# Layer 1 with its projections token-major, gates turned by TensorE, and six places for split weights

## The chip, the cores and the metric

The kernel runs on one core of one Trainium2 chip, as one launch. A core has five engines with a queue each, which take their instructions in order: TensorE (PE in the profile, its weight loads PEld), VectorE (DVE), ScalarE (ACT), GpSimd (POOL) and SyncE (SP), which here issues DMAs. The metric is the device time of that core in microseconds, the median of several runs.

## The reference, cut to what matters

Two layers over 256 latent tokens and 256 context tokens of width 2048, all in float32. Layer 0 runs neighbourhood attention and a bidirectional state-space scan and is not changed. Layer 1 is a short gated convolution over the latent tokens:

```python
shift, scale, gate = adaln(c, ada_w[i], ada_b[i])
h = modulate(rms_norm(x, norm_g[i]), shift[:, None], scale[:, None])
...
def short_conv_mixer(h, w_in, conv_w, w_out):
    p = h @ w_in
    bg, cg, hv, g = jnp.split(p, 4, axis=-1)
    y = bg * dw_conv(cg * hv, conv_w)
    return (jax.nn.silu(g) * y) @ w_out
...
x = x + gate[:, None] * y
```

`w_in` is 2048 x 8192 here, `w_out` 2048 x 2048, and `dw_conv` has three taps along the tokens for each channel.

## The kernel before

[...] Weights arrive in chunks of 512 KB (two blocks of 128 input channels by 512 columns) in a `raw` buffer (L377); ACT rounds them to the high part `wH` (L407), DVE subtracts for the low part `wL` (L414). There are three places for split chunks; `split` may run at most three chunks ahead of the use.

The program is written out in an order that the kernel works out while it is built. The main code emits the matmuls of a projection chunk by chunk and calls `pump` between them; side work stands in generators in the queues `urgent`, `side` and `back`. A generator yields what it needs (an engine and the tiles it reads, or a condition), and `pump` emits its next piece when the model `Plan` says that the engine will be free and the tiles ready. `force` emits until a condition holds. What comes out is one fixed order for each engine, which the chip runs in order; where the model was too hopeful an engine waits.

Two forms of projection are used. In the form "act" (`mm_act`) a block of activations, 128 channels by 128 tokens, is the stationary operand and 512 columns of weights stream through: tokens end up on the partitions, in one bank for each of the two token tiles, with three matmuls of 512 columns per block and tile. In the form "both" (`mm_both`) a block of weights, 128 channels by 128 columns, is stationary, and the high and low activations of all 256 tokens, side by side, stream through: 512 columns with the high weights, then 256 (high activations only) with the low weights. Channels end up on the partitions, with high and low terms in two halves of a bank that are added while it is evicted.

- Output projection of layer 0 ("act"): 32 blocks of `mix` by four column blocks of 512, in three passes. At its last pass the last three chunks (`NTAIL` 13 of 16) are run first for token tile 0, then for tile 1, so that the rows of tile 0 can be evicted early. `res_gen` (L1582 to L1589) multiplies by the gate, adds x to give `x1`, and sums the squares on ACT.
- Entry to layer 1. `turn_gen` turns `x1` to channel-major, two blocks at a time, by eight pieces of four transposes (L193), and multiplies by the norm's weight. `norm_gen` makes the factor of the norm for each tile (L1652, and POOL L1653), spreads it over the partitions by a transpose, and for each of 16 blocks multiplies (L1681 or L1683), rounds with the shift added (ACT L1688) and takes the rest (DVE L1669), for both token tiles together. `keep_up` gives PE 8 and 6 transposes of a constant to do. Layer 1's matmuls begin when the first blocks of both tiles are there. While `hold` is set no further weights are split but where `norm_gen` does so.
- Input projection of layer 1 ("both"): for each of four groups of 512 channels, the parts cg, hv, bg, g, four banks each, 16 blocks by four column blocks. Evictions: `both` copies one half (ACT L1771) and adds the other (DVE L1773); `hv_gen` multiplies by cg and runs the three taps along the free axis (L1786 to L1794); `bg_gen` multiplies (L1801); `gg_gen` does the gate by tanh (L1810 to L1814) and splits the product into `y2` (L1818, L1819).
- Output projection of layer 1 ("act"), evicted by `fin_gen` (L1840, L1842) with a store for each tile.
- In the background the modulation of layer 1 is computed from `ada_w` by DVE (L804, `acc`), with a few small matmuls; the last 36 of its 256 steps on DVE fall into layer 1's input projection.

Of the kernel before, what the change touches and what calls it, by code (L numbers as in the profile page):

```python
# [141 lines left out]
def kernel(ctx: ExitStack, tc, x, cx, ada0, ada_w, ada_b, w_in, w_out, sc_in, sc_out, rpb, small, const,  # L142
# [245 lines left out]

    def split():
        k = pos["split"]  # L390
        raw, v = RAW.pop(k)
        nb, n = v.shape[1], v.shape[2]
        if n == 64:

            while lows:
                low_part()
            W = WH[k % NW].rearrange("p (b c) -> p b c", b=nb)
# [7 lines left out]
        H = WH[k % NW][:, :nb * n].rearrange("p (b c) -> p b c", b=nb)  # L405
        Lo = WL[k % NW][:, :nb * n].rearrange("p (b c) -> p b c", b=nb)
        E(S.copy(H, v))  # L407
        lows.append((k, H, Lo, v, raw))
        pos["split"] += 1
# [13 lines left out]
    def split_half(b):  # L423
# [5 lines left out]
        def rest():  # L429
            E(V.tensor_tensor(out=Lo[:, b], in0=v[:, b], in1=H[:, b].bitcast(F32), op=ALU.subtract))  # L430
            if b:
                RAW.pop(0)
                HL[0] = (H, Lo)
                pos["split"] += 1
                give_raw(raw)
                issue()
# [3 lines left out]
    def splits_try():  # L440
# [3 lines left out]
        while pos["split"] < pos["use"] + NW and pos["split"] in RAW:  # L444
# [18 lines left out]
    def used():  # L463
        pos["use"] += 1
        splits_try()
# [78 lines left out]
    for i in range(4):  # L544
        for part in (1, 2, 0, 3):
# [104 lines left out]
    def mm_both(ps, act, H, Lo, first, last):  # L650

        for b, o in enumerate(ps):
            bb = slice(b * 128, (b + 1) * 128)
            mm(o, H[:, bb], act, first, False)
            mm(o[:, :256], Lo[:, bb], act[:, :256], False, last)
            if b % 2:
                pump()

    def chunk(kb0, kind, ps, first, last, lhs=None):
# [3 lines left out]
        for j in range(nb):  # L663
# [5 lines left out]
            elif kind == "both":  # L669
                mm_both(ps, aH, H[:, j], Lo[:, j], f, l)  # L670
# [896 lines left out]
    def res_gen(k, c0, ps):  # L1567
# [31 lines left out]
    rb1 = []  # L1599
# [5 lines left out]
    def turn_gen():  # L1605
        yield when(lambda: n_back[0] >= 11.5 and attn[0] == 32 and ssd_done[0] == 8)
        for k in range(2):
            pt = st([128, 4, 256], f"PT{k}", name=f"late{k}")
            late[4 * k:4 * k + 4] = [pt[:, q, :] for q in range(4)]
        E(V.scalar_tensor_tensor(out=A1, in0=M1[:, 1], scalar=1.0, in1=P_("g1"), op0=ALU.add, op1=ALU.mult))  # L1610
        for kp in range(0, KB, 2):
# [6 lines left out]
            if kp == 14:  # L1618
                keep_up(8)
                yield when(lambda: ("sq", 3, 1) in got)  # L1620
# [12 lines left out]
    def keep_up(n):  # L1633

        pt = bank()
        for _ in range(n):
            turn(pt[:, :128], ident)
        give(free_b, pt)

    s3 = st([128, 2], "s3")  # L1640

    def norm_gen():
# [4 lines left out]
        rb = None  # L1647
        for t in range(2):
            yield when(lambda: ("sq", 3, t) in got)
            yield W_("DVE", ss1[:, t])  # L1650
# [3 lines left out]
            ahead = t == 0 and pos["split"] < pos["use"] + NW and pos["split"] in RAW  # L1654
            if ahead:
                split()
            if ahead:
                while lows:
                    low_part()

            yield W_("PE", r, nb=0 if t else 1)
            if t == 0:
                rb = bank()
            turn(rb[:, t * 128:(t + 1) * 128], r.to_broadcast([128, 128]))
        keep_up(6)
        hls = {}

        def low(kb):
            E(V.scalar_tensor_tensor(out=hls[kb][:, 1], in0=late[kb], scalar=S1[:, kb:kb + 1], in1=hls[kb][:, 0].bitcast(F32),  # L1669
                                     op0=ALU.add, op1=ALU.subtract))  # L1670
            hL[kb] = hls[kb][:, 1]
            h1[kb] = hls[kb].rearrange("p a b -> p (a b)")


        base = pos["use"]
        r2 = None
        for kb in range(KB):
            yield when(lambda: ("turn", kb) in got and (kb < 6 or pos["use"] >= base + kb // 2 - 2))
            yield W_("DVE", rb if r2 is None else r2, held[kb] if kb in held else late[kb])
            if kb not in held:  # L1680
                E(V.tensor_tensor(out=late[kb], in0=late[kb], in1=rb[:, :256] if r2 is None else r2, op=ALU.mult))  # L1681
            else:
                E(V.scalar_tensor_tensor(out=late[kb], in0=held[kb][:, (kb % 2) * 256:(kb % 2) * 256 + 256], scalar=A1[:, kb:kb + 1],  # L1683
                                         in1=r2, op0=ALU.mult, op1=ALU.mult))
                if kb % 2:
                    give(free_b, held[kb])
            hls[kb] = st([128, 2, 256], f"hL{kb}", F32R, name=f"h1_{kb}")
            E(S.activation(hls[kb][:, 0], late[kb], AF.Identity, bias=S1[:, kb:kb + 1], scale=1.0))  # L1688
            if kb:
                low(kb - 1)  # L1690
            while lows and kb in (3, 5):
                low_part()
            if kb == 3:
                r2 = half()
                E(S.copy(r2, rb[:, :256]))
                give(free_b, rb)
            if kb in (1, 3) and pos["split"] < pos["use"] + NW and pos["split"] in RAW:
                split()
        low(KB - 1)
        give(free_h, r2)  # L1700

    NTAIL = 13
    kcol = 0
    for ns in ((0, 512), (1024,), (1536,)):
        pss = [banks(2) for n in ns]
        for ip in range(16):
# [8 lines left out]
            if hold[0]:  # L1715
# [4 lines left out]
                ws = [use(q) for q in range(16 - NTAIL)]  # L1720
                spawn(urgent, norm_gen(), 0, 1)
                for t in range(2):
                    for q, (H, Lo) in enumerate(ws):
                        for b in range(2):
                            i = 2 * order[NTAIL + q] + b
                            mm_act([pss[0][t]], mH[i][:, 0, t * 128:(t + 1) * 128], mH[i][:, 1, t * 128:(t + 1) * 128],
                                   H[:, b], Lo[:, b], False, NTAIL + q == 15 and b == 1)
# [8 lines left out]
        if len(ns) == 2:  # L1736
            force(lambda: attn[0] == 32 and not side)
            x1 += [st([128, D], "KT", name="x1a"), st([128, D], "Vt", name="x1b")]
            spawn(side, turn_gen())
# [10 lines left out]
    force(lambda: hL[1] is not None, (urgent,))  # L1750
    hold[0] = False
    pump()
# [4 lines left out]
    flat = lambda ap, b: ap[:, 2 * b:2 * b + 2, :].rearrange("p b c -> p (b c)")  # L1757
    cg, u, v = st([128, 4, 256], "gt", name="cg"), st([128, 4, 256], "sz", name="u"), st([128, 4, 256], "QT", name="v")
# [3 lines left out]
    def ordered(k, gen):  # L1762
        yield when(lambda: seq[0] == k)
        yield from gen
        seq[0] += 1

    def both(p, o=None):

        yield W_("ACT", p)
        o = half() if o is None else o  # L1770
        E(S.copy(o, p[:, 256:]))  # L1771
        yield W_("DVE", o)
        E(V.tensor_tensor(out=o, in0=p[:, :256], in1=o, op=ALU.add))  # L1773
        give(free_b, p)
        return o

    def cg_gen(i, ps):
        for b in range(4):
            yield from both(ps[b], cg[:, b, :])

    def hv_gen(i, ps):
        for b in range(4):
            ch = 4 * i + b
            yield from both(ps[b], u[:, b, :])
            yield W_("DVE", u[:, b, :])
            E(V.tensor_tensor(out=u[:, b, :], in0=u[:, b, :], in1=cg[:, b, :], op=ALU.mult))  # L1786
            yield W_("ACT", u[:, b, :])
            E(S.mul(v[:, b, :], u[:, b, :], scw[:, 1, ch:ch + 1]))
        for b in range(4):
            ch = 4 * i + b  # L1790
            yield W_("DVE", v[:, b, :])
            E(V.scalar_tensor_tensor(out=v[:, b, 1:256], in0=u[:, b, 0:255], scalar=scw[:, 0, ch:ch + 1], in1=v[:, b, 1:256],
                                     op0=ALU.mult, op1=ALU.add))
            E(V.scalar_tensor_tensor(out=v[:, b, 0:255], in0=u[:, b, 1:256], scalar=scw[:, 2, ch:ch + 1], in1=v[:, b, 0:255],  # L1794
                                     op0=ALU.mult, op1=ALU.add))

    def bg_gen(i, ps):
        for b in range(4):
            bg = yield from both(ps[b])
            yield W_("DVE", bg, v[:, b, :])  # L1800
            E(V.tensor_tensor(out=v[:, b, :], in0=bg, in1=v[:, b, :], op=ALU.mult))  # L1801
            give(free_h, bg)

    def gg_gen(i, ps):
        for b in range(4):
            kb = 4 * i + b
            gg = yield from both(ps[b])
            yield W_("ACT", gg)
            th = half()
            E(S.activation(th, gg, AF.Tanh, scale=0.5))  # L1810
            yield W_("DVE", v[:, b, :])
            E(V.tensor_tensor(out=v[:, b, :], in0=gg, in1=v[:, b, :], op=ALU.mult))
            yield W_("DVE", th)
            E(V.scalar_tensor_tensor(out=v[:, b, :], in0=th, scalar=1.0, in1=v[:, b, :], op0=ALU.add, op1=ALU.mult))  # L1814
            give(free_h, gg, th)
            yield W_("ACT", v[:, b, :])
            hl = st([128, 2, 256], f"hH{kb}", F32R, name=f"y2_{kb}")
# [95 lines left out]
```

## Time and profile before

| | us |
|---|---|
| median of 3 runs | 1796.73 (1795.94 to 1799.53) |
| profiled execution | 1797.29 |
| its span, first to last instruction | 1795.5 |
| granted TensorE clock, mean | 1.000 |
| first matmul of layer 1's input projection | 1337.51 |
| first matmul of its output projection | 1701.90 |

Times within the trace are microseconds from the span's start. In a row of the timeline stand start, length, engine, line, operation, output <- inputs, shapes and count; in brackets the idle time of the engine before it and what ended it. Matmuls of a run overlap in the trace (each is listed with its latency), so their cost is the distance from one start to the next.

### The profile page before, as it was taken

To read this page: it belongs to the slowest core of one execution; us is meant where nothing else is said; L and a number is where in the kernel's file an instruction comes from. 1 tells how busy PE (TensorE), PEld (TensorE's weight loads), DVE (VectorE), ACT (ScalarE), POOL (GpSimd) and SP (SyncE) were. 2 spreads that over 40 slices of the span, in tenths; PEclk is the share of its full clock that TensorE was granted. 3 is DMA by queue.
4 is the path that set the end of the run, shared out by engine and by line. 5 is a ranking of instruction groups with operands and counts; after the bars stand their busy time and mean duration, and the time that the engine had idled before them with its cause. 6 is when DMAs were issued, how large, how long until landed. Compare 5 with 4: busy or idle time off the path is not lost. (4 is left out here: it accounts for less than half of the span.)

```text
span 1795.5 us, 26501 instructions
## 1 busy us (share of the span) xinstructions
PE 1765.5 (98%) x10039; PEld 1490.7 (83%) x10039; DVE 1292.8 (72%) x2073; ACT 786.9 (44%) x1386; POOL 32.5 (2%) x28
## 2 busy tenths in 40 slices
PE   6999999999999999999999999999999999999998
PEld 4677988879888889888888898788888888888887
DVE  5656787888676878676877688786667877565665
ACT  5323544455242445242435344555444444444442
POOL 0000100001000000000001000000000000000000
PEclk9999999999999999999999999999999999999999
DMA  9987744666746665745764567657766786666564
GB/s 359 339 285 239 225 143 125 204 183 200 235 127 202 211 185 175 232 139 173 218 200 134 165 185 247 202 186 268 274 222 225 249 265 222 185 185 187 186 213 150
DMA packets 222368, 374.67 MB, mean 209 GB/s; under 512 B 32432, under 2 KB 69136, under 8 KB 222240
## 3 DMA queue, kind: packets, MB, share of 16 engines
q1 hardware_dynamic: 214928, 366.38, 64.0%
q10 hardware_dynamic: 7312, 6.61, 1.1%
q8 instruction: 78, 1.28, 0.3%
q14 instruction: 50, 0.41, 0.1%
HBM read 367.52 MB, written 6.72 MB: 208 GB/s over the span
## 5 line engine op out<-in xcount | busy, mean ns | idle before, releaser
L407 ACT CAST wH<-raw 128x1024 fp32r<-128x1024 f32 (+1 forms) x439 | 457.8, 1044 | 687.3 <-PE bank L189 561.3
L414 DVE TENSOR_TENSOR wL<-raw,wH 128x1024 fp32r<-128x1024 f32 (+1 forms) x439 | 531.5, 1214 | 250.0 <-ACT wH L407 247.2
L189 PE MATMUL bank<-h,wH 128*128 128x512 f32 x1024 | 362.5, 399 | 1.4 <-DVE h L1669 0.9
L189 PE MATMUL bank<-hH,wH 128*128 128x256 f32 (+1 forms) x1040 | 343.3, 330 | 0.8 <-ACT wH L407 0.8
L189 PE MATMUL bank<-hL,wH 128*128 128x256 f32 (+1 forms) x1040 | 338.0, 325 | 0.0
L189 PE MATMUL bank<-hH,wL 128*128 128x256 f32 (+1 forms) x1024 | 330.8, 323 | 0.8 <-DVE wL L414 0.6
L189 PE MATMUL bank<-h,wL 128*128 128x256 f32 x1024 | 287.6, 281 | 0.0
L189 PE MATMUL bank<-wH,hH 128*128 128x512 f32 x640 | 257.1, 402 | 3.9 <-ACT hH L744 2.6
L189 PE MATMUL bank<-wL,hH 128*128 128x512 f32 x640 | 250.4, 392 | 0.0
L189 PE MATMUL bank<-wH,hL 128*128 128x512 f32 x640 | 249.8, 391 | 0.1
L804 DVE SCALAR_TENSOR_TENSOR acc<-raw,csil,acc 128x512 f32<-128x512 f32 x256 | 191.8, 749 | 63.2 <-DMA raw<-in_ada_w 54.3
L189 PEld LDWEIGHTS bank<-h,wH 128*128 128x128 f32 x1024 | 192.4, 188 | 50.4 <-issue 1.5
L189 PEld LDWEIGHTS bank<-hH,wH 128*128 128x128 f32 x1040 | 196.5, 189 | 18.6 <-ACT wH L407 1.3
L189 PEld LDWEIGHTS bank<-hL,wH 128*128 128x128 f32 x1040 | 196.8, 189 | 15.5
L189 PEld LDWEIGHTS bank<-hH,wL 128*128 128x128 f32 x1024 | 194.0, 189 | 18.3 <-DVE wL L414 1.6
L189 PEld LDWEIGHTS bank<-h,wL 128*128 128x128 f32 x1024 | 193.4, 189 | 0.0
L189 PE MATMUL bank<-wH,mix 128*128 128x512 f32 x512 | 163.1, 393 | 1.1 <-DVE Vt L998 1.1
L189 PEld LDWEIGHTS bank<-wH,hH 128*128 128x128 f32 x640 | 120.2, 188 | 33.8 <-issue 5.0
L189 PEld LDWEIGHTS bank<-wH,hL 128*128 128x128 f32 x640 | 120.2, 188 | 26.1 <-DVE hL L750 0.6
L189 PEld LDWEIGHTS bank<-wL,hH 128*128 128x128 f32 x640 | 120.2, 188 | 24.7 <-DVE wL L430 0.5
L189 PEld LDWEIGHTS bank<-wH,mix 128*128 128x128 f32 x512 | 96.1, 188 | 21.7 <-DVE Vt L998 1.6
L189 PE MATMUL bank<-wL,mix 128*128 128x512 f32 x256 | 100.0, 391 | 0.3 <-DVE wL L414 0.3
(262 smaller groups left out, 1764.0 us busy)
## 6 DMA issues: line engine op xcount, KB each, us to landing
raw<-in_w_in SPq DMA_DIRECT2D x208, 512.0 KB
raw<-in_ada_w SPq DMA_DIRECT2D x128, 512.0 KB
raw<-in_sc_in SPq DMA_DIRECT2D x128, 512.0 KB
raw<-in_w_out SPq DMA_DIRECT2D x64, 512.0 KB
raw<-in_ada SPq DMA_DIRECT2D x37, 512.0 KB
raw<-in_sc_out SPq DMA_DIRECT2D x32, 512.0 KB
tmp<-dram_csr SPq DMA_DIRECT2D x32, 256.0 KB
PT<-in_ada SPq DMA_DIRECT2D x14, 512.0 KB
```

The source lines that it names most:

```text
L189: E(T.matmul(o, l, r, start=start, stop=stop, skip_group_check=True))
L407: E(S.copy(H, v))
L414: E(V.tensor_tensor(out=Lo, in0=v, in1=H.bitcast(F32), op=ALU.subtract))
L804: E(V.scalar_tensor_tensor(out=acc, in0=v[:, j], scalar=csil[:, 2 * k + j:2 * k + j + 1], in1=acc, op0=ALU.mult, op1=ALU.add))
```

## The change

The same sums of products are computed. The parts of layer 1's input projection change form, order and eviction; its entry is cut by token tiles; the number of places for split weights becomes six from the second of the three passes of layer 0's output projection on.

- Places are handed out from a list `free_w` and return when a chunk is used. The three new ones lie in tiles that are free by then: `KL`, `QT` with `QL`, and `gt` with `sz`.
- The input projection runs in the form "act", two banks for each part, in the order cg, hv, g, bg. cg is copied by ACT, hv multiplied by it on DVE, the gate is made from g (tanh on ACT, one multiply-add on DVE), all with tokens on the partitions. `over` turns the products by four transposes into one bank for two column blocks: u before the taps, and bg times the gate before it meets the taps' output.
- At the entry the first eight blocks are scaled, rounded and split for token tile 0 alone and layer 1's first 48 matmuls run on it; then the same for tile 1. Blocks 8 to 15 follow for both tiles, two at a time. The eviction of the second tile's rows of `x1` waits for "first". The transpose that spreads the first factor is emitted after 15 of the 18 last matmuls of tile 1 (`NSTOP`). `keep_up` is gone.

```diff
+    free_w, in_use = deque(range(NW)), deque()
+    def place():
+        in_use.append(free_w.popleft())
+        return in_use[-1]
...
-        while pos["split"] < pos["use"] + NW and pos["split"] in RAW:
+        while free_w and pos["split"] in RAW:
...
-        for part in (1, 2, 0, 3):
+        for part in (1, 2, 3, 0):
             q_proj(sc_in, part * D + i * 512, 512)
...
-            yield when(lambda: x1 and (k in passed or ("rows", k, t) in got))
+            yield when(lambda: x1 and (k in passed or ("rows", k, t) in got) and (k < 3 or t == 0 or "first" in got))
...
+        def scaled(kb, tt):
+            o = pts[kb // 4][:, kb % 4:kb % 4 + 2, tt]
+            E(V.tensor_tensor(out=o, in0=o, in1=rb[0][:, tt].unsqueeze(1).to_broadcast([128, 2, 128]), op=ALU.mult))
+            high(kb, tt)
+            high(kb + 1, tt)
...
+        yield from factor(0)
+        ahead()
+        yield from spread(0)
+        tt = slice(0, 128)
+        yield W_("DVE", rb[0][:, tt])
+        scaled(0, tt)
+        scaled(2, tt)
+        for kb in range(0, 4):
+            low(kb, tt)
+        scaled(4, tt)
+        got.add("first")
+        yield when(lambda: ("sq", 3, 1) in got)
+        low(4, tt)
+        low(5, tt)
+        scaled(6, tt)
+        yield from factor(1)
+        if lows:
+            low_half(0)
+        low(6, tt)
+        low(7, tt)
...
+        yield from spread(1)
...
+        yield from pair(8)
+        for kp in range(8, KB, 2):
+            if lows:
+                low_part()
+            low(kp, slice(0, 256))
+            low(kp + 1, slice(0, 256))
+            if kp < KB - 2:
+                yield from pair(kp + 2)
...
+            for H, Lo in ((KL[:, 0:2], KL[:, 2:4]), (QT, QL), (st([128, 4, 256], "gt", F32R, name="wH5"), st([128, 4, 256], "sz", F32R, name="wL5"))):
+                free_w.append(len(WH))
...
+    def over(rows_, b):
+        yield W_("PE", *rows_, nb=1)
+        pt = bank()
+        for k in range(2):
+            for t in range(2):
+                turn(pt[:, k * 256 + t * 128:k * 256 + (t + 1) * 128], rows_[t][:, (b + k) * 128:(b + k + 1) * 128])
+        return pt
...
+    def bg_gen(i, ps):
+        for t in range(2):
+            yield W_("DVE", ps[t])
+            E(V.tensor_tensor(out=sg[t], in0=ps[t], in1=sg[t], op=ALU.mult))
+            give(free_b, ps[t])
+        for b in range(0, 4, 2):
+            pt = yield from over(sg, b)
+            yield W_("DVE", pt)
+            E(V.tensor_tensor(out=flat(v[:, b:b + 2, :]), in0=pt, in1=flat(v[:, b:b + 2, :]), op=ALU.mult))
...
     for i in range(4):
-        for part, gen in ((1, cg_gen), (2, hv_gen), (0, bg_gen), (3, gg_gen)):
-            ps = banks(4)
...
-                chunk(kb, "both", ps, kb == 0, kb == KB - 2, lambda i: (h1[i], None))
+        for part, gen in ((1, cg_gen), (2, hv_gen), (3, gg_gen), (0, bg_gen)):
+            ps = banks(2)
...
+                chunk(kb, "act", ps, kb == 0, kb == KB - 2, lambda i: h1[i])
```

In the order written out for PE, 512 matmuls and the 14 transposes of `keep_up` are gone and 64 transposes are added; the order is the same up to the beginning of the second pass of layer 0's output projection. SP issues the same number of loads.

More of the change, by code (lines that the diff above doesn't have):

```diff
@@ L392, in split @@
         nb, n = v.shape[1], v.shape[2]
+        w = place()
         if n == 64:
@@ L1618, in turn_gen @@
             if kp == 14:
-                keep_up(8)
-                yield when(lambda: ("sq", 3, 1) in got)
+                yield when(lambda: ("h1", 7, 0) in got)
             for b in range(2):
@@ L1646, in norm_gen, with factor @@
         E(V.tensor_scalar(out=s3, in0=s3, scalar1=D * EPS, scalar2=None, op0=ALU.add))
-        rb = None
-        for t in range(2):
+        rb = []
+        hls = {}
+        def factor(t):
             yield when(lambda: ("sq", 3, t) in got)
+            if t == 0:
+                behind()
             yield W_("DVE", ss1[:, t])
@@ L1653, in norm_gen, with ahead, behind, low_half @@
             E(G.tensor_tensor(out=r, in0=r, in1=mhalf[:, :1], op=ALU.pow))
-            ahead = t == 0 and pos["split"] < pos["use"] + NW and pos["split"] in RAW
-            if ahead:
+        def ahead():
+            if free_w and pos["split"] in RAW:
                 split()
-            if ahead:
-                while lows:
-                    low_part()
+        def behind():
+            while lows:
+                low_part()
+        def low_half(b):
+            k, H, Lo, v, raw = lows[0]
+            E(V.tensor_tensor(out=Lo[:, b], in0=v[:, b], in1=H[:, b].bitcast(F32), op=ALU.subtract))
+            if b:
+                lows.popleft()
+                HL[k] = (H, Lo)
+                give_raw(raw)
+                issue()
@@ L1661, in norm_gen, with spread @@
+        def spread(t):
+            r = r1[:, t:t + 1]
             yield W_("PE", r, nb=0 if t else 1)
             if t == 0:
[L1663 to L1672, printed above, removed]
@@ L1675, in norm_gen @@
[L1675 to L1691, printed above, removed]
-                low_part()
[L1693 to L1698, printed above, removed]
@@ L1699, in norm_gen, with low @@
-        low(KB - 1)
+                rb.append(bank())
+            turn(rb[0][:, t * 128:(t + 1) * 128], r.to_broadcast([128, 128]))
+            got.add(("r", t))
+        def low(kb, tt):
+            E(V.scalar_tensor_tensor(out=hls[kb][:, 1, tt], in0=late[kb][:, tt], scalar=S1[:, kb:kb + 1],
+                                     in1=hls[kb][:, 0, tt].bitcast(F32), op0=ALU.add, op1=ALU.subtract))
+            for t in range(2):
+                if tt.start <= t * 128 < tt.stop:
+                    got.add(("h1", kb, t))
@@ new lines, in high @@
+        def high(kb, tt):
+            if kb not in hls:
+                hls[kb] = st([128, 2, 256], f"hL{kb}", F32R, name=f"h1_{kb}")
+                h1[kb] = (hls[kb][:, 0], hls[kb][:, 1])
+            E(S.activation(hls[kb][:, 0, tt], late[kb][:, tt], AF.Identity, bias=S1[:, kb:kb + 1], scale=1.0))
+        def scaled(kb, tt):
[3 more added lines that the diff above has]
+            high(kb + 1, tt)
@@ new lines, in pair @@
+        def pair(kp):
+            yield when(lambda: ("turn", kp + 1) in got)
+            yield W_("DVE", r2, held[kp] if kp in held else late[kp])
+            for kb in (kp, kp + 1):
+                if kb not in held:
+                    E(V.tensor_tensor(out=late[kb], in0=late[kb], in1=r2, op=ALU.mult))
+                else:
+                    E(V.scalar_tensor_tensor(out=late[kb], in0=held[kb][:, (kb % 2) * 256:(kb % 2) * 256 + 256],
+                                             scalar=A1[:, kb:kb + 1], in1=r2, op0=ALU.mult, op1=ALU.mult))
+                high(kb, slice(0, 256))
+            if kp in held:
+                give(free_b, held[kp])
+            ahead()
@@ new lines, in norm_gen @@
+        low(7, tt)
+        if lows:
+            low_half(1)
+        yield from spread(1)
+        tt = slice(128, 256)
+        yield W_("DVE", rb[0][:, tt])
+        scaled(0, tt)
+        scaled(2, tt)
+        for kb in range(0, 4):
+            low(kb, tt)
+        scaled(4, tt)
+        scaled(6, tt)
+        r2 = half()
+        E(S.copy(r2, rb[0][:, :256]))
+        ahead()
+        for kb in range(4, 8):
+            low(kb, tt)
+        give(free_b, rb[0])
+        yield from pair(8)
@@ L1720 @@
                 ws = [use(q) for q in range(16 - NTAIL)]
+                while lows:
+                    low_part()
+                if free_w and pos["split"] in RAW:
+                    split()
                 spawn(urgent, norm_gen(), 0, 1)
                 for t in range(2):
+                    done_ = 0
                     for q, (H, Lo) in enumerate(ws):
@@ L1797, in bg_gen @@
-    def bg_gen(i, ps):
[L1798 to L1817, printed above, removed]
-            E(S.copy(hl[:, 0], v[:, b, :]))
-            E(V.tensor_tensor(out=hl[:, 1], in0=v[:, b, :], in1=hl[:, 0].bitcast(F32), op=ALU.subtract))
-            y2[kb] = hl
@@ L1822 @@
-    for i in range(4):
-        for part, gen in ((1, cg_gen), (2, hv_gen), (0, bg_gen), (3, gg_gen)):
-            ps = banks(4)
-            for kb in range(0, KB, 2):
-                force(lambda: hL[kb + 1] is not None)
-                chunk(kb, "both", ps, kb == 0, kb == KB - 2, lambda i: (h1[i], None))
-            spawn(urgent, ordered(4 * i + (1, 2, 0, 3).index(part), gen(i, ps)), 0, {0: 1, 3: 2}.get(part, 0))
+        if k < 2:
+            budget[0] -= 2
+        if k == 13:
+            budget[0] += 4
+            give(free_t, *cg, *u)
@@ new lines, in ordered @@
+        seq[0] += 1
+    def over(rows_, b):
[5 more added lines that the diff above has]
+        return pt
+    def cg_gen(i, ps):
+        for t in range(2):
+            yield W_("ACT", ps[t])
+            if i == 0:
+                cg.append(tmp())
+            E(S.copy(cg[t], ps[t]))
+            give(free_b, ps[t])
@@ new lines, in hv_gen @@
+    def hv_gen(i, ps):
+        for t in range(2):
+            yield W_("DVE", ps[t])
+            if i == 0:
+                u.append(tmp())
+            E(V.tensor_tensor(out=u[t], in0=ps[t], in1=cg[t], op=ALU.mult))
+            give(free_b, ps[t])
+        for b in range(0, 4, 2):
+            pt = yield from over(u, b)
+            yield W_("ACT", pt)
+            for k in range(2):
+                ch = 4 * i + b + k
+                E(S.mul(v[:, b + k, :], pt[:, k * 256:k * 256 + 256], scw[:, 1, ch:ch + 1]))
+            for k in range(2):
+                ch, o = 4 * i + b + k, k * 256
+                yield W_("DVE", v[:, b + k, :])
+                E(V.scalar_tensor_tensor(out=v[:, b + k, 1:256], in0=pt[:, o:o + 255], scalar=scw[:, 0, ch:ch + 1],
+                                         in1=v[:, b + k, 1:256], op0=ALU.mult, op1=ALU.add))
+                E(V.scalar_tensor_tensor(out=v[:, b + k, 0:255], in0=pt[:, o + 1:o + 256], scalar=scw[:, 2, ch:ch + 1],
+                                         in1=v[:, b + k, 0:255], op0=ALU.mult, op1=ALU.add))
+            give(free_b, pt)
@@ new lines, in gg_gen @@
+    def gg_gen(i, ps):
+        for t in range(2):
+            yield W_("ACT", ps[t])
+            E(S.activation(sg[t], ps[t], AF.Tanh, scale=0.5))
+            yield W_("DVE", sg[t])
+            E(V.scalar_tensor_tensor(out=sg[t], in0=sg[t], scalar=1.0, in1=ps[t], op0=ALU.add, op1=ALU.mult))
+            give(free_b, ps[t])
+    def bg_gen(i, ps):
+        for t in range(2):
+            yield W_("DVE", ps[t])
+            E(V.tensor_tensor(out=sg[t], in0=ps[t], in1=sg[t], op=ALU.mult))
+            give(free_b, ps[t])
+        for b in range(0, 4, 2):
+            pt = yield from over(sg, b)
+            yield W_("DVE", pt)
+            E(V.tensor_tensor(out=flat(v[:, b:b + 2, :]), in0=pt, in1=flat(v[:, b:b + 2, :]), op=ALU.mult))
+            give(free_b, pt)
+            yield W_("ACT", v[:, b:b + 2, :])
+            for k in range(2):
+                kb = 4 * i + b + k
+                hl = st([128, 2, 256], f"hH{kb}", F32R, name=f"y2_{kb}")
+                E(S.copy(hl[:, 0], v[:, b + k, :]))
+                yield W_("DVE", hl[:, 0])
+                E(V.tensor_tensor(out=hl[:, 1], in0=v[:, b + k, :], in1=hl[:, 0].bitcast(F32), op=ALU.subtract))
+                y2[kb] = hl
```

92 lines of the change are left out of this document (42 added, 50 removed).

## The prediction

> **What bounds the kernel now.** First the page: which engine is busy, and at which clock.
>
> ```profile
> span 1795.5 us, 26501 instructions
> ...
> PE 1765.5 (98%) x10039; PEld 1490.7 (83%) x10039; DVE 1292.8 (72%) x2073; ACT 786.9 (44%) x1386; POOL 32.5 (2%) x28
> ...
> PEclk9999999999999999999999999999999999999999
> ```
>
> PE is idle for only 30 us, so the time is the sum of PE's instructions and what is saved must be saved on PE. Then the chain of waits, which says what the end hangs on:
>
> ```profile
> 1722.73 66.83 PE bank L189 x291
> 1789.56 0.02 issue
> 1789.58 0.70 DVE tmp L1840
> ...
> 1791.64 0.69 DVE tmp L1842
> ```
>
> Matmuls without a break, then the last eviction and its store. Third, busy time by stretches that I cut at the first and last instruction of a stage: the entry to layer 1, its input projection, its output projection.
>
> ```profile
> core 0: us, PE busy (x) PEld busy (x) DVE busy (x) ACT busy (x) POOL busy (x), PEclk, DMA share, GB/s
> 1331.41:1337.51 6.10, 4.57 (x37) 3.90 (x36) 3.98 (x8) 2.65 (x7) 0.56 (x1) 1.00 0.29 86
> 1337.51:1701.90 364.39, 363.90 (x2080) 314.57 (x2081) 254.54 (x357) 171.40 (x244) 0.00 (x0) 1.00 0.67 211
> 1290.07:1330.28 40.21, 40.21 (x179) 33.23 (x177) 25.46 (x28) 16.43 (x20) 0.00 (x0) 1.00 0.82 286
> ```
>
> The projection is 364.39 us with 0.49 idle; DVE has 110 us left in it and ACT 193. The DMA share is 0.67, and 0.82 in the output projection of layer 0 (last row), where PE still had no gap. So neither DMA, DVE nor ACT bounds these stages; PE's instruction stream does. Busy times of single groups of matmuls are not to be added: instructions overlap, and only the distance from start to start is a cost.
>
> **Part 1, the form of the projection's matmuls.** Before, each of 4 x 4 x 16 x 4 weight blocks costs a pair: 512 columns (`h,wH`), then 256 (`h,wL`). After, each of 4 x 4 x 16 x 2 tile steps costs three of 512 columns, as in both output projections. 786,432 columns either way, in 2048 instructions before and 1536 after.
>
> ```profile
> L189 PE MATMUL bank<-h,wH x1024: 391/398/501, 1337.5 to 1701.6; 128*128 128x512 f32 x171
> ...
> 1356.92 0.40 PE L189 MATMUL bank<-h,wH 128*128 128x512 f32 x1
> 1357.16 0.28 PE L189 MATMUL bank<-h,wL 128*128 128x256 f32 x1
> ...
> 1361.51 0.40 PE L189 MATMUL bank<-h,wH 128*128 128x512 f32 x1
> ...
> 1376.09 0.64 PE L189 MATMUL bank<-acc,const 128*32 128x128 f32 x16
> 1376.67 0.50 PE L189 MATMUL bank<-h,wH 128*128 128x512 f32 x1
> ...
> 1701.90 0.40 PE L189 MATMUL bank<-wH,y 128*128 128x512 f32 x1
> ...
> 1789.84 0.39 PE L189 MATMUL bank<-wH,y 128*128 128x512 f32 x1
> ```
>
> From 1337.51 to 1701.90 are 364.39 us. Off go the 0.49 idle and two groups of 16 small `acc` matmuls (1376.09 to 1376.67, and some 0.1 at the switch: 0.7 each), which stay. 362.5 us are left for 1024 pairs, 0.354 each; the 13 pairs from 1356.92 to 1361.51 confirm it (4.59 / 13 = 0.353). The new form has two prices in this trace: in the output projection of layer 1, 383 steps from 1701.90 to 1789.84, 0.2296 us; in that of layer 0, 177 steps (the 179 of the window less its two edges) in 40.21 us, 0.2272. 1536 of them are 349.0 to 352.7. I take the middle, 351.0, since the new stage evicts as the first does and loads nearly as the second. Gain 11.5 us (9.8 to 13.5).
>
> [...]
>
> **Part 2, 64 transposes more.** Conv inputs and gates are now token-major and are turned in 16 groups of four (`over`: two for each `hv_gen`, two for each `bg_gen`, four column blocks). The trace has this shape in the same stream:
>
> ```profile
> 1181.52 0.39 PE L189 MATMUL bank<-wH,mix 128*128 128x512 f32 x1
> 1181.75 0.60 PE L193 MATMUL bank<-const,tmp 128*128 128x128 f32 x4
> 1182.11 0.48 PE L189 MATMUL bank<-wH,mix 128*128 128x512 f32 x1
> 1182.42 0.39 PE L189 MATMUL bank<-wL,mix 128*128 128x512 f32 x1
> ```
>
> From 1181.75 to 1182.42 are 0.67 us; less one matmul's 0.23, four transposes cost 0.44, switch included. 16 times this is 7.0 us (5.8 if the slow matmul behind them, 0.08 each, were not theirs). They also add a wait: PE takes its queue in order, so a transpose whose product is late holds up every matmul of the running part behind it. The waits of PE from 1200 us on (us in total, times, longest) show how well the recorded order places such work:
>
> ```profile
> PE bank L189 <- DVE h L1669: 0.9, 1, 0.9
> PE bank L189 <- DVE half L1435: 0.7, 1, 0.7
> PE bank L193 <- DVE x1b L1585: 0.6, 1, 0.6
> PE bank L189 <- ACT h L1688: 0.5, 1, 0.5
> ```
>
> One wait at a transpose in all of that, 0.6 us, at a forced place. The floor for the 16 groups is 0, the ceiling 0.6 each, 9.8 us; below nothing is excluded, as a wait saves nothing. I take 0.2 in all: these groups come while a part of 22 us runs, and can be put anywhere in it.
>
> **Part 3, the entry to layer 1.**
>
> ```profile
> 1331.98 0.39 PE L189 MATMUL bank<-wH,mix 128*128 128x512 f32 x1
> 1332.21 0.27 PE L193 MATMUL bank<-const,x1a 128*128 128x128 f32 x1
> ...
> 1333.97 0.33 PE L193 MATMUL bank<-const,x1b 128*128 128x128 f32 x1 [0.61 <-DVE x1b L1585]
> ...
> 1337.51 0.50 PE L189 MATMUL bank<-h,wH 128*128 128x512 f32 x1 [0.92 <-DVE h L1669]
> ...
> 1348.15 0.47 PE L189 MATMUL bank<-h,wH 128*128 128x512 f32 x1 [0.49 <-ACT h L1688]
> ...
> 1328.21 0.69 DVE L1582 TENSOR_TENSOR tmp<-bank,tmp 128x512 f32<-128x512 f32 x1 [1.49 <-DMA raw<-in_sc_in]
> ...
> 1330.42 0.21 DVE L1652 TENSOR_SCALAR r<-ss,s 128x1 f32<-128x1 f32 x1 [0.79 <-ACT tmp L1589]
> ...
> 1333.22 0.69 DVE L1585 TENSOR_TENSOR x1b<-tmp,tmp 128x512 f32<-128x512 f32 x1
> ...
> 1335.97 0.75 DVE L1681 TENSOR_TENSOR late<-late,bank 128x256 f32<-128x256 f32 x2 [1.05 <-PE bank L193]
> ...
> 1339.12 1.22 DVE L414 TENSOR_TENSOR wL<-raw,wH 128x1024 fp32r<-128x1024 f32 x1
> ...
> 1342.45 0.48 DVE L1669 SCALAR_TENSOR_TENSOR h<-late,M,h 128x256 fp32r<-128x256 f32 x1
> ```
>
> Without layer 1's matmuls PE spends 1332.21 to 1337.51, 5.30 us, and 0.49 at 1348.15: 5.79. The 16 turns of x1 and the turn of the second factor stay: 17 at 0.11 is 1.87. The 14 idle turns of `keep_up` (1.5), the 0.61 and the 0.92 can go. New waits, worked along the chain. From L1582 at 1328.21 to the turn of the first factor at 1331.41 (the start of the window above) are 3.2 us, as now. Then the first tile is scaled two blocks at a time (256 elements, 0.4 by L1681), ACT rounds and DVE takes the rest (128 elements, 0.3, an estimate from L1669's 0.48 for 256): the first high half stands at about 1332.6, its rest at 1333.0, and PE has three `mix` matmuls and eight turns to do until 1333.1. Covered. The second tile's eviction waits on DVE for "first", behind three scalings and four rests: it starts near 1334.3 in place of 1332.50, x1b stands at 1335.7 in place of 1333.9, and PE asks for it at 1335.8. Its factor is there 3.2 us after 1334.3, at 1337.5, and PE asks 8 turns and 3 matmuls after 1335.8, at 1337.3: some 0.3 late, and behind it stand all of the tile's matmuls. Later, in the chunks of blocks 8 to 15, DVE has one L414 (1.14 to the next start) and four steps of 0.41: 2.8 us against PE's 12 x 0.2285 = 2.7. DVE only keeps step, and I allow 0.4. After: 1.9 + 0.3 + 0.4 = 2.6. Gain 3.2 us; 3.9 with no wait, 0 if DVE falls a whole chain behind.
>
> **What costs nothing.** Three more places let splits of weights run ahead; PE waited for no split after 1200 us (the waits above), so nothing is to be had there. SP issues as many loads in a new order, weights ahead of `ada_w`; the DVE work on those makes the last gate, which is first used when the output projection is evicted. Fewer and wider evictions replace the 64 `both` adds: PE does not see it as long as DVE keeps 110 us of slack. Without that cover, what DVE does late is the price of the transposes' wait above. The tail, from the last part to `y2`, has 12 blocks of output projection (16 us) before it.
>
> **Sum.** The profiled execution took 1797.29, its span and 1.8 around it. 1797.3 - 11.5 + 7.0 + 0.2 - 3.2 = 1789.8. It stood 0.56 above the median of the runs, so the forecast is 1789.3, 0.4% faster.
>
> **Rivals.**
> (a) The entry gains nothing: DVE, with two half-width passes for each block, is the new wait there, and the 3.2 are spent. For: it has 2.8 us of work for 2.7 of matmuls. Against: six split places give a head start. 1792.5 to 1793.
> (b) PE waits at the transposes. Price 0.6 for each of 16 groups, from the one such wait above: 1789.3 + 9.6 = 1798.9. It turns the sign from 0.47 us a group (7.5 / 16). For: DVE has L414 of 1.2 us in its queue at any time, and waits for `ada_w` in it. Against: the same kind of transposes in layer 0.
> (c) Columns are the price: the pair's extra is not of its form but of what runs beside it in layer 1, so 512 columns go on costing 0.354 x 512 / 768 = 0.236. Then part 1 gains nothing: 1789.3 + 11.5 = 1800.8, slower. For: equal columns. Against: the layer-0 stage with the DMA at 0.82 had 0.227. [...]
>
> **How the numbers follow.** Forecast 0.70, (a) 0.15, (b) 0.09, (c) 0.06. The bounds of the three parts give 1785.5 at best (13.5 gain, 5.8 transposes, 3.9 entry, no wait: 11.6 off). Upward I reach through (a) with the dearer matmul price (1.7 more) and some waits: 1795.5; (b) and (c) stay out. 0.2% is 3.6 us, about what can be told from no change here. Faster takes the forecast and a third of (a): 0.75. Same 0.14: the rest of (a) and small (b). Slower 0.11.
>
> **What will show it.** Matmuls of the new projection 0.227 to 0.230 apart; L193 groups of four 0.44 with no idle noted; under 3 us of non-matmul time between the last `mix` and a steady layer 1. The prediction falls if the projection stage is 362 us or more, if idle before L193 passes 5 us, or if PE's idle at the entry passes 3 us.

## The result, and the profile after

The change makes the kernel faster: 1783.91 us median of 6 runs (1781.73 to 1789.31) against 1796.14 before (1795.94 to 1799.53), ratio 0.9937, 95% interval 0.9927 to 0.9946. The forecast was 1789.3, range 1785.5 to 1795.5: the right sign, too small a size, and the time lies 1.6 us under the range.

First the page of the changed kernel, then its busy time from the first matmul of layer 1's input projection to the first of its output projection (columns as in the prediction).

```profile
span 1782.2 us, 25428 instructions
...
PE 1755.5 (99%) x9577; PEld 1470.5 (83%) x9577; DVE 1265.6 (71%) x1986; ACT 773.7 (43%) x1330; POOL 32.2 (2%) x28
```

```profile
core 0: us, PE busy (x) PEld busy (x) DVE busy (x) ACT busy (x) POOL busy (x), PEclk, DMA share, GB/s
1330.89:1688.49 357.60, 357.57 (x1636) 295.53 (x1635) 235.71 (x287) 162.78 (x200) 0.94 (x1) 1.00 0.68 219
```

The stage shrank from 364.39 to 357.60 us although it now holds 56 of the 64 turns and half of the entry's turns of x1. In the list of PE's waits of the changed kernel nothing stands from 1200 us on. The timeline of PE shows the entry and the steps:

```profile
1329.87 0.39 PE L189 MATMUL bank<-wH,mix 128*128 128x512 f32 x1
1330.10 0.27 PE L193 MATMUL bank<-const,x1a 128*128 128x128 f32 x1
...
1330.89 0.48 PE L189 MATMUL bank<-wH,h 128*128 128x512 f32 x1
...
1333.71 0.27 PE L193 MATMUL bank<-const,x1a 128*128 128x128 f32 x1
...
1334.50 0.47 PE L189 MATMUL bank<-QT,h 128*128 128x512 f32 x1
...
1335.04 0.40 PE L189 MATMUL bank<-QT,h 128*128 128x512 f32 x1
1335.47 0.32 PE L193 MATMUL bank<-const,r 128*128 128x128 f32 x1
1335.55 0.48 PE L189 MATMUL bank<-QT,h 128*128 128x512 f32 x1
...
1342.03 0.39 PE L189 MATMUL bank<-wL,h 128*128 128x512 f32 x1
...
1350.87 0.39 PE L189 MATMUL bank<-wL,h 128*128 128x512 f32 x1
...
1424.45 0.27 PE L193 MATMUL bank<-const,sgH 128*128 128x128 f32 x1
...
1424.81 0.47 PE L189 MATMUL bank<-wH,h 128*128 128x512 f32 x1
1425.12 0.39 PE L189 MATMUL bank<-wL,h 128*128 128x512 f32 x1
...
1688.49 0.39 PE L189 MATMUL bank<-QT,y 128*128 128x512 f32 x1
...
1776.66 0.39 PE L189 MATMUL bank<-wH,y 128*128 128x512 f32 x1
```

The last `mix` matmul ends its turn at 1330.10, layer 1 starts at 1330.89 (before: 1332.21 and 1337.51). The 39 steps from 1342.03 to 1350.87 are 0.2267 us apart. A group of four turns, 1424.45 to 1425.12 less one step, costs 0.44. The second factor comes 0.2 late (1335.04 to 1335.47 where a step takes 0.23).

The two profiled spans differ by 13.3 us, but 2.1 of these are no work of the change. Up to the beginning of the second pass of layer 0's output projection PE's order is the same in both kernels, and the first turn of x1, 8.9 us into that pass in both, comes at 1252.0 before and at 1249.9 after (the view of the tile x1a of the changed kernel):

```profile
L193 PE MATMUL bank<-const,x1a x16: 270/273/273, 1249.9 to 1334.4; 128*128 128x128 f32 x16
```

So the profile shows some 11.2 us for the change, about what the ratio says (0.63% of 1796 is 11.3). The experiments below were read in the same way, by the stretch from the first turn of x1 to the first matmul of layer 1's output projection:

| kernel | first turn of x1 | first `y` matmul | between |
|---|---|---|---|
| before | 1252.0 | 1701.9 | 449.9 |
| after | 1249.9 | 1688.5 | 438.6 |
| e1 form alone | 1254.4 | 1697.8 | 443.4 |
| e2 form and places | 1254.6 | 1702.2 | 447.6 |
| e3 places alone | 1252.3 | 1702.3 | 450.0 |
| e4 change again | 1252.6 | 1691.2 | 438.6 |

### The profile page after: what moved, and what is told of

It is laid out like the page before. It is cut to its first block, busy times and chain, and to the rows that moved or that the text cites. A ratio compares the mean times of both kernels' runs of the same rounds, so it can differ in the third digit from the quotient of the medians.

```text
span 1782.2 us, 25428 instructions
## 1 busy us (share of the span) xinstructions
PE 1755.5 (99%) x9577; PEld 1470.5 (83%) x9577; DVE 1265.6 (71%) x1986; ACT 773.7 (43%) x1330; POOL 32.2 (2%) x28
## 4 chain that ended last, share of the span: by engine, by line
PE 93%; DMA 3%; DVE 2%; ACT 1%; issue 0%; POOL 0%; SPq 0%; ACTq 0%; DVEq 0%
PE bank L189 90%; PE bank L193 3%; DMA tmp<-dram_csr 1%; DVE wL L421 1%; DMA raw<-in_ada 0%; DMA tmp<-dram_exr 0%; DVE mix L1546 0%; DMA tmp<-dram_mixd 0%; DMA const<-in_const 0%; ACT wH L414 0%; DVE tmp L744 0%; DMA raw<-in_w_out 0%; DVE tmp L1388 0%; DVE hL L748 0%; DVE tmp L1399 0%
## 5 line engine op out<-in xcount | busy, mean ns | idle before, releaser
L414 ACT CAST wH<-raw 128x1024 fp32r<-128x1024 f32 (+1 forms) x375 | 390.8, 1044 | 595.0 <-PE bank L189 515.9
L421 DVE TENSOR_TENSOR wL<-raw,wH 128x1024 fp32r<-128x1024 f32 (+1 forms) x374 | 452.2, 1212 | 214.3 <-ACT wH L414 212.4
L189 PE MATMUL bank<-wH,h 128*128 128x512 f32 x680 | 215.6, 391 | 0.0
L189 PEld LDWEIGHTS bank<-hL,wH 128*128 128x128 f32 x1040 | 196.8, 189 | 15.5
L189 PEld LDWEIGHTS bank<-wH,h 128*128 128x128 f32 x680 | 127.7, 188 | 26.5 <-issue 0.2
L189 PE MATMUL bank<-wH,mix 128*128 128x512 f32 x432 | 138.8, 393 | 1.1 <-DVE Vt L996 1.1
L189 PE MATMUL bank<-wL,h 128*128 128x512 f32 x340 | 132.3, 389 | 0.0
L189 PEld LDWEIGHTS bank<-wH,mix 128*128 128x128 f32 x432 | 81.1, 188 | 18.7 <-DVE Vt L996 1.5
L189 PE MATMUL bank<-wL,mix 128*128 128x512 f32 x216 | 84.4, 391 | 0.3 <-DVE wL L421 0.3
L189 PEld LDWEIGHTS bank<-wL,h 128*128 128x128 f32 x340 | 63.9, 188 | 12.9
```

The lines of the kernel that those rows point to most:

```text
L189: E(T.matmul(o, l, r, start=start, stop=stop, skip_group_check=True))
L421: E(V.tensor_tensor(out=Lo, in0=v, in1=H.bitcast(F32), op=ALU.subtract))
```

## The experiments

**The change taken apart.** e1 keeps the new projection and gives back the old entry (both tiles together, `keep_up`) and three places; e2 has six places; e3 is the kernel before with six places (three work tiles of its evictions lie elsewhere for it); e4 is the change again. All ran on one chip with the kernel before, which took 1798.12 us there (24 runs). The diffs show parts of the edits.

```diff
e1, against after
-            for H, Lo in ((KL[:, 0:2], KL[:, 2:4]), (QT, QL), ...
-                free_w.append(len(WH))
...
-        yield from factor(0)
-        ahead()
-        yield from spread(0)
...
+        for kb in range(KB):
+            yield when(lambda: ("turn", kb) in got and (kb < 6 or pos["use"] >= base + kb // 2 - 2))
...
-            if i == 0 and part == 1:
+            if False:
e3, against before
-        while pos["split"] < pos["use"] + NW and pos["split"] in RAW:
+        while free_w and pos["split"] in RAW:
...
-    cg, u, v = st([128, 4, 256], "gt", name="cg"), st([128, 4, 256], "sz", name="u"), st([128, 4, 256], "QT", name="v")
+    cg, u, v = st([128, 4, 256], "PT0", name="cg"), st([128, 4, 256], "PT1", name="u"), st([128, 4, 256], "Btm", name="v")
```

> Layer 1's projection token-major with turned products, but the entry as before (both token tiles together, 14 idle turns) and three places. My theory, with the step prices of the changed kernel: 1536 steps of 0.227 us in place of 1024 pairs of 0.354 save 13.8 us, 64 turns at 0.11 cost 7.0: 6.8 us faster than before, about 1789.3; the first matmul of layer 1 some 5.3 us after the last of layer 0, as before. Rival 'columns are the price': no gain from the form, 7 us slower than before. Rival 'the form needs the new entry or the places to keep PE fed': less than 4 us faster, with idle time of PE before layer 1's matmuls or turns.

> The same with six places for split weights, entry still as before. My theory: the places bring nothing, since PE waited for no split weight after 1200 us: within 0.7 us of the form alone. Rival 'the places carry the 2.1 us that the changed kernel is ahead before layer 1 begins': 2 us faster than the form alone, all of it before the last matmul of layer 0.

> The kernel before with six places for split weights and nothing else (three work tiles of layer 1's evictions lie elsewhere for it). My theory: within 0.7 us of before. Rival: 2 us faster, before layer 1 begins. Third reading, that the 2.1 us are chance between executions: the time at which the second pass of layer 0's output projection begins, where the order of PE is still that of before, differs by 1 to 2 us between these four kernels with no relation to what was changed.

> The changed kernel once more, beside the three parts. My theory: form 6.8 and entry 3.7 add to 10.5 us under before, about 1785.7, and 1 to 2 us of the 12.2 measured were chance ahead of the change. Rival 'all of 12.2 is the change': 12 us again, and the place where the order first differs is reached 2 us earlier again.

| | median us | ratio to before | 95% interval |
|---|---|---|---|
| e1 form alone | 1791.91 | 0.9968 | 0.9956 to 0.9979 |
| e2 form and places | 1792.53 | 0.9972 | 0.9963 to 0.9981 |
| e3 places alone | 1796.89 | 0.9999 | 0.9990 to 1.0008 |
| e4 change again | 1786.72 | 0.9936 | 0.9924 to 0.9949 |

The form brings 0.32% (5.8 us; 6.5 in the table of stretches). The places bring nothing, by themselves (e3) or added to the form (e2). The rest, 443.4 to 438.6 or 4.8 us in the profiles, goes to the new entry; this is a subtraction, since the entry was not run without the places. It is 1.1 more than the entry's gain worked out below. Some 0.5 of this are slower steps behind the old kernel's waits, which are not counted there: its first 64 pairs took 23.65 us (1337.51 to 1361.16), 0.49 of it idle, where 64 pairs elsewhere took 22.61. The other 0.6 is that the old entry does not quite keep the new form fed. e1's list of PE's waits has two that layer 1's first matmuls meet:

```profile
PE bank L189 <- ACT h L1687: 0.4, 1, 0.4
PE bank L189 <- DVE wL L421: 0.2, 1, 0.2
```

Its first 96 steps take 23.95 us (1339.37 to 1363.32), against 23.15 in the changed kernel, which has nine turns among them. So the rival that needs the entry or the places to keep PE fed holds for about half a microsecond and falls as an account of the gain. "Columns are the price" falls too. The third reading of e3 is borne out: the first turn of x1 came between 1249.9 and 1254.6 us in kernels whose order up to there is the same but for the split places, and the change itself met it at 1249.9 and, as e4, at 1252.6. e2's profile has a wait the others lack. DVE stood behind a load of `ada_w`, the eviction was late, and PE waited at a turn; then, in the busy time by stretches, the granted clock was 0.51 over 3.4 us:

```profile
1522.91 1.54 DVE L802 SCALAR_TENSOR_TENSOR acc<-raw,csil,acc 128x512 f32<-128x512 f32 x2 [3.30 <-DMA raw<-in_ada_w]
...
1525.50 0.68 DVE L1829 TENSOR_TENSOR sgH<-bank,sgH 128x512 f32<-128x512 f32 x1
...
1526.24 0.33 PE L193 MATMUL bank<-const,sgH 128*128 128x128 f32 x1 [1.51 <-DVE sgH L1829]
```

```profile
1528.00:1531.40 3.40, 3.40 (x11) 2.43 (x9) 2.42 (x4) 1.66 (x3) 0.00 (x0) 0.51 0.75 254
```

This is the prediction's rival (b), in one group of one execution (1797.7 us, the slowest of e2's twelve; its median shows nothing of it).

**The price of a turn, and of its place.** e5 runs each group of four twice into the same bank. e6 puts it into PE's queue at once. These two, and e7 and e8, ran on another chip, where the kernel before took 1796.89 us (19 runs).

```diff
e5
+        for _ in range(2):
             for k in range(2):
                 for t in range(2):
                     turn(pt[:, k * 256 + t * 128:k * 256 + (t + 1) * 128], ...
e6
-        yield W_("PE", *rows_, nb=1)
+        yield when(lambda: free_b)
```

> The change with each of its 16 groups of four turns run twice into the same bank. My theory, that a turn costs PE 0.11 us and nothing else, at full price since PE has no free time: the projection stage 16 x 0.44 = 7.0 us longer, the kernel 4.4 us under before in place of 11.4. Rival 'the turns lie in gaps of the matmul stream': under 2 us more. Rival 'a turn costs its listed 0.272 us': 17 us more, slower than before.

> The change, but each group of turns is put into PE's queue as soon as its product is put into DVE's, without regard to when that product will be ready. My theory: what keeps the turns cheap is their place. PE then waits in eight parts (hv and bg of four column groups) for an eviction that takes two products of 0.69 us after the part's last matmul: some 1.6 us each, 13 us in all, so slower than before by 1 to 2 us, with idle time before L193 of 10 us or more. Rival 'DVE is far enough ahead': no more than 2 us, no idle noted before L193.

Busy time of the projection stage of e5, then of e6:

```profile
1333.93:1697.61 363.68, 363.68 (x1693) 301.57 (x1692) 236.41 (x287) 163.34 (x200) 0.94 (x1) 1.00 0.68 216
```

```profile
1333.09:1706.22 373.13, 364.51 (x1641) 297.79 (x1639) 238.19 (x289) 164.04 (x201) 0.94 (x1) 0.99 0.66 210
```

e5: 0.9978 (0.9969 to 0.9987), 1792.85 us. Its stage holds 14 of the 16 groups and is 6.08 us longer than the change's, 0.434 a group, with PE busy throughout: a turn costs its distance of 0.11 us at full price, neither nothing nor the 0.272 that a row lists. e6: 1.0019 (1.0009 to 1.0029), 1800.92 us: the whole gain and more is gone. Its stage is 15.5 us longer with 8.6 idle, and the waits are at the turns:

```profile
PE bank L193 <- DVE tmp L1866: 4.1, 7, 1.8
PE bank L193 <- DVE sgL L1894: 2.5, 4, 1.6
PE bank L193 <- DVE sgH L1894: 1.9, 4, 1.0
```

It was expected 1 to 2 us slower than before and came some 4 slower, though the waits were shorter than expected (8.5, not 13). Two stretches at about half clock behind the longest of them (0.57 granted from 1429 to 1432 us, 0.58 from 1476 to 1480) add some 3.4. The other 3.5 were not traced; a part of it must be that idle time counts from a matmul's listed end, 0.39 us behind its start, where the next would have started 0.23 behind. The place in the queue is what makes the turns cheap: no wait at a turn in the changed kernel, 8.5 us of them here.

**What the steps cost.** e7 is the kernel before with 512 columns for the low weights too, which adds the product of low by low. e8 moves the stationary operands of the last projection to other tiles. Each was run once, so only their profiles are read, not their totals.

```diff
e7, against before
-            mm(o[:, :256], Lo[:, bb], act[:, :256], False, last)
+            mm(o, Lo[:, bb], act, False, last)
e8, against after
-                hl = st([128, 2, 256], f"hH{kb}", F32R, name=f"y2_{kb}")
+                hl = st([128, 2, 256], f"hH{(kb + 8) % 16}", F32R, name=f"y2_{kb}")
```

> The kernel before, where the matmul with the low weights also streams 512 columns (it adds the product of low by low). Theory 'the short step is dear': a step of 512 costs 0.227 in this form too, the pair 0.454, the stage 1024 x 0.454 + 1.9 = 467 us (before: 364). Rival 'the form is dear' (a new stationary block of weights for each step): the 14 ns that a pair costs above 768 columns at the price of the new form stay, 0.468 a pair, 481 us.

> The change with the stationary operands of the last projection moved: block kb lies in the tile of block kb + 8 (modulo 16). In the changed kernel the steps of blocks 0 to 7 took 0.229 us and those of 9 to 14 0.2267. Theory 'the price hangs on where the operand lies': now blocks 8 to 15 take 0.229 and 0 to 6 0.2267. Rival 'it hangs on what the other engines do at that time of a column block': blocks 0 to 7 stay the slower ones. No change in total under either.

e7 in the timeline of PE, and by stretches:

```profile
1360.27 0.39 PE L189 MATMUL bank<-h,wL 128*128 128x512 f32 x1
1360.50 0.39 PE L189 MATMUL bank<-h,wH 128*128 128x512 f32 x1
...
1362.99 0.39 PE L189 MATMUL bank<-h,wL 128*128 128x512 f32 x1
```

```profile
1339.49:1805.54 466.05, 466.05 (x2081) 385.09 (x2081) 257.29 (x357) 173.82 (x245) 0.00 (x0) 1.00 0.55 165
```

12 steps in 2.72 us, 0.2267 each, in the old form: expected 467, measured 466.05. So the form with weights stationary is not dear by itself; the pair with a step of 256 columns is: it costs 0.354 where the same 768 columns in steps of 512 cost 0.340. Why is left open.

For e8 one column block of the output projection, first of the change, then of e8; the first row is step 0 (block 0), the second step 49 (block 8), the third step 72 (block 12).

```profile
1755.02 0.39 PE L189 MATMUL bank<-QT,y 128*128 128x512 f32 x1
...
1766.23 0.39 PE L189 MATMUL bank<-wL,y 128*128 128x512 f32 x1
...
1771.44 0.39 PE L189 MATMUL bank<-QT,y 128*128 128x512 f32 x1
```

```profile
1755.16 0.39 PE L189 MATMUL bank<-QT,y 128*128 128x512 f32 x1
...
1766.27 0.39 PE L189 MATMUL bank<-wL,y 128*128 128x512 f32 x1
...
1771.53 0.39 PE L189 MATMUL bank<-QT,y 128*128 128x512 f32 x1
```

The change: 11.21 us for 49 steps, 0.2288 each, then 0.2265. e8: 0.2267, then 0.2287. The dear steps went where their tiles went. For 48 steps that is 0.11 us, so some 0.4 us in the four column blocks.

**A safer place for the turns.** e9 emits them 3 us later by the model's clock, e10 is the change beside it, on a third chip (before: 1796.63 us, 11 runs).

```diff
e9
+        yield when(lambda: plan.ready(rows_) + 3000 <= plan.t["PE"])
         yield W_("PE", *rows_, nb=1)
```

> The change, with each group of turns put 3 us (by the model of the order) later into PE's queue than it is now. In e2 one group waited 1.5 us because DVE stood 3.3 us behind a load of ada_w; in the change's own profile no group waited, in e8 one for 0.4. Theory: the turns are placed late enough already, and the wait is an accident of some executions worth a microsecond: ratio to before within 0.001 of the change's 0.9936, no wait before L193 in the profile. Rival 'such waits cost every execution 1 to 3 us': ratio 0.992 or less. Against it, products that stay 3 us longer in banks could hold up matmuls: then over 0.995 and idle before L189.

> The change beside e9 on the same chip: 0.9936 again, 11 to 12 us under before; the projection stage 357.6 us; the place where PE's order first differs is reached anywhere from 1248 to 1254 us.

e9: 0.9938 (0.9926 to 0.9950), 1785.22 us, no wait in its list; e10: 0.9937 (0.9925 to 0.9949), 1785.46 us, one wait of 0.3 at a turn, and a stage of 358.45 us where 357.6 was expected. The two can't be told apart: the turns stand late enough, and no version run here beats the change by more than the noise.

## Why the prediction was right in sign and off in size

The mechanism held: PE's instruction stream is the bound (busy 357.57 of the stage's 357.60 us), the same columns cost less in steps of 512 (768 columns 0.340 us in them, 0.354 as a pair), and turns cost their distance (0.11 us). The sum gave 7.5 us of the 11.2 in the profiles. The terms below account for 3.5 of the 3.7 that it lacked.

- **Part 1, the form: the mis-sized term.** "I take the middle, 351.0" was the step that failed. After takes 357.60 less 14 groups (6.2), eight turns of x1 (0.9), the second factor (0.3) and the two `acc` groups (1.4): 348.9 us for 1536 steps, 0.2271. That is the price of layer 0's projection, the lower end. Gain 13.6 in place of 11.5. The upper end, 0.2296, came from the output projection of layer 1, and the prediction took its extra for what evictions beside the stream cost. Above 0.2267 a step, the extra is 1.1 us over the 383 steps, and the traces place most of it elsewhere. Some 0.4 belongs to the tiles in which blocks 0 to 7 of `y` lie (e8). Another 0.40 is one interruption in the kernel before, from 1722.21 to 1723.06, where two steps took 0.85 us:

```profile
1722.28 0.40 ACT L1818 CAST y<-v 128x256 fp32r<-128x256 f32 x1
...
1722.73 0.50 PE L189 MATMUL bank<-wH,y 128*128 128x512 f32 x1
1723.06 0.40 PE L189 MATMUL bank<-wL,y 128*128 128x512 f32 x1
```

  PE starts here 0.05 us behind the end of ACT's last `y`, so it probably waited for that. And 0.21 lies in the 48 steps from 1724.23 to 1735.43, 0.2333 each, with no cause shown.
- **Equal columns, under part 1.** That equal columns cost the same in either form holds for steps of 512, by e7 (0.2267 us with weights stationary, and 0.2267 in the changed kernel), and fails for the pair with 256, by the kernel before (0.354 against 0.340). The gain of the form lies in that difference alone.
- **Part 2, the turns:** 7.0 predicted, 0.434 a group in e5, so 6.9. No wait at a turn in the profile; 0.2 had been allowed.
- **Part 3, the entry:** 3.2 predicted. Before 5.79; after 0.79 (1330.10 to 1330.89), 0.79 (1333.71 to 1334.50), 0.28 at the second factor, and 0.26 in all for the slower steps behind the three (0.31 in place of 0.23): 2.1, so 3.7. (The 0.5 of slower steps behind the old kernel's waits stays, as in the prediction, in part 1.) The late factor cost 0.2, near the 0.3 worked out; the 0.4 allowed for DVE in blocks 8 to 15 never came, since DVE kept step (no wait of PE there).
- **Not in the sum:** the output projection. From 1688.49 to 1776.66 are 88.17 us with two groups of turns in them; less 0.88 it is 87.3 where before took 87.94, a gain of 0.6 that the prediction put at nothing. It is the interruption at 1722.21 (0.40) and the slow steps behind 1724.23 (0.21): the changed kernel has neither, and nor have e1 and e4. The dear steps of blocks 0 to 7 cost the same in both kernels (0.2288 in the last column block of each).
- **Rivals.** (a) fell: no wait at the entry. (b) is real but rare with the planned places (longest wait 1.5 us in e2, 0.4 in e8, 0.3 in e10), and e6 shows its price (8.5 us of waits). (c) fell in the profile after and in e7 (0.2267 a step, not 0.236).
- **The range.** Its lower end took the best of each part, 11.6 under the forecast's base of 1796.8: that is 1785.2, not the 1785.5 written. The parts as they came, 11.2, lead to about 1785.5, the very edge. That five of the six runs of the result lie under it took chance as well: the profiled one reached the first turn of x1 2.1 us before the old kernel did, and the range left no room for that scatter. Later sets of the change took 1786.72 and 1785.46.

## What to carry to other kernels

Before choosing which operand is stationary, price the actual steps from the trace, start to start: here the same columns cost 4% more when a third of them came in steps of 256 (0.354 us against 0.340), enough to pay for 64 turns and leave more than 6 us. A helper transpose on the full engine cost its distance here, 0.11 us (e5), and nothing else, with its input ready when PE got there; put at once into the queue the 64 of them cost more than the whole change brought (e6: 1800.92 us, before 1796.89). And entering a stage by halves of the rows turned 5.8 us without its matmuls into 2.1.

## What the runs showed of the hardware

- **Half clock behind some waits.** In e1 PE waited 1.7 us for a DVE product in layer 0, and the next 3.4 us ran at a granted clock of 0.50; e2 had 3.4 us at 0.51, and e6 4 us at 0.58. Busy time of e1 by stretches:

```profile
1209.00:1212.00 3.00, 1.60 (x9) 1.43 (x10) 2.96 (x6) 0.82 (x1) 0.37 (x1) 1.00 0.87 232
1212.00:1215.40 3.40, 3.40 (x11) 2.63 (x10) 1.54 (x3) 0.35 (x1) 1.23 (x1) 0.50 1.00 348
```

  The loss is 1.7 us each time. The executions before and after had none of it: every 3.4 us of theirs up to the last matmul was at 1.00. How long PE stands idle does not decide it alone. In e3 PE was idle for 2.48 of 3.00 us, more than ahead of any of these, and the clock stayed at 1.00:

```profile
1138.90:1141.90 3.00, 0.52 (x3) 0.47 (x3) 2.79 (x8) 2.68 (x7) 0.00 (x0) 1.00 0.67 223
1141.90:1145.30 3.40, 3.40 (x16) 2.77 (x16) 3.19 (x8) 3.37 (x8) 0.00 (x0) 1.00 0.49 139
```

  What does decide it is open. In e1 such a stretch lies ahead of the first turn of x1 and can explain 1.7 us of its late arrival there.
- **A step's price hangs on the tile of its stationary operand:** 0.2288 against 0.2266 for the same instruction (e8). One execution each; what in the place does it was not tried.
- **Turns do not slow their neighbours** beyond 0.08 us at the switch, doubled or not, in the group read in each: the first matmul behind it took 0.31 us in place of 0.23 (1424.81 to 1425.12 in the changed kernel, 1429.16 to 1429.47 in e5), the next 0.23 and 0.24.
